# A table builder's back step cut in two inside an expert loop: four transposes move ahead of the second half of the token gathering

## Chip, cores and metric

The kernel runs on one core of a Trainium2 chip. The metric is device time in microseconds (us) of one execution; lower is better. Engines are named as in the profile: PE is TensorE's matmul, PEld its weight load, DVE is VectorE, ACT ScalarE, POOL GpSimd, SP SyncE, whose queue issues most of the transfers.

## The reference, cut to what matters

Two transformer blocks run one after the other on 512 tokens of width 1024. The first ends in a mixture of 32 experts, of which each token takes two; the second has an S5 layer (a state space model over 64 groups), whose tables follow from small parameters alone.

```python
y = (jax.nn.silu(xb @ w_gate[e]) * (xb @ w_up[e])) @ w_down[e]   # one expert; gate and up 1024x512, down 512x1024
...
b_bar = ((lam_bar - 1) / lam)[..., None] * lax.complex(b_re, b_im)   # S5, per group
a_pow = jnp.exp(lam_dt[None] * steps)
y = jnp.einsum('btgp,ghp->btgh', hs, c_mat).real
```

## The kernel before

**Expert stage.** `moe` walks through eight steps `st` of four experts, two pairs `pr` each, so 16 pairs; `eA` is the first expert of a pair and is 0 only for the first. For a pair PE makes the gate and up products `G` and `U` (L1032), turns the one-hot matrix (`pohT`, L1055), gathers tokens for the next step, turns the hidden values `hm` (`phT`, L1064, copied by ACT to `hT`, L1066), and makes the down products `Y` (L1081). The parts of the previous pair's result (`combine`, tile `pcmb`, L996 and L997) lie between the products. The first pair gathers nothing ahead, the second gathers four quarters, the pairs of the last step none, and each of the others two quarters: one before `phT` and one behind it. A quarter is 16 matmuls into one PSUM tile `pg` (L943, L944), which ACT moves out in two instructions to `xg` (L947). `pohT`, `pg` and `phT` take turns in a pool of two PSUM buffers.

**Weights.** SP issues them in the order of the program. A pair's ten tiles of 1 MB go through a ring of eight buffers (L129), and two more go to fixed places (`extra`, L970). A tile's transfer waits until the buffer's last reader on PE is done, and what is behind it on SP waits too: the last two `up` tiles of a pair wait for the `Y` before it.

**S5 tables.** The generator `s5_blocks` builds them in 16 half-blocks, in the shadow of the experts. Each half-block has three steps that end in a `yield`: loads by POOL (`Bd`, `cr`, `dd`, L1592 to L1597); maps (two small transposes `pcd`, and DVE's products `pb` and `m3`, which the profile names `m`); and the back step. The back step turns `pb` in four transposes into the PSUM tile `pm2` (L1628, `pm` in the profile), which ACT copies to `me` (L1629); then eight small products `pkt` (L1635) and one with the diagonal `dd` (L1637) go into a second tile, ACT copies that to `kt` (L1639), and POOL stores `me`, `m3` and `kt` (L1640 to L1642). `pm2` and `pkt` are taken from the same pool `psz` of one PSUM buffer, so the first `pkt` product waits for the copy of `pm2`.

**What sets the order.** In the expert stage PE's order is that of the program text: `pin` ties each matmul to the one before. On the other engines a scheduler orders by a simulation of its own and may take an instruction ahead of the text, as it does with DVE's product on `dd` (L1632). `pre` calls `next(self.blocks)` four times, so that half-block 0 is done and the loads of half-block 1 are out. The first pair then takes one step (maps of 1). Each pair after it takes two steps between the second quarter and `Y` (back, and the loads of the next half-block) and one behind `Y` (maps).

Of the kernel before, what the change touches and what calls it, by code (L numbers as in the profile page):

```python
# [71 lines left out]
def bcast_rows(ap, n):  # L72

    return bass.AP(tensor=ap.tensor, offset=ap.offset, ap=[[0, n]] + [list(x) for x in ap.ap])
# [24 lines left out]
class Build:  # L99
# [304 lines left out]
    def pre(self):  # L404
# [135 lines left out]
        for _ in self.side:  # L540
            pass
        self.ada_ctx.close()
        for _ in range(4):
            next(self.blocks)
        late = self.B((128, 4, D), name="late")
        g1 = late[:, 0]
# [402 lines left out]
    def moe(self):  # L949
# [29 lines left out]
        with ExitStack() as cx:  # L979
# [33 lines left out]
            for st in range(8):  # L1013
# [4 lines left out]
                for pr in range(2):  # L1018
                    eA = e0 + 2 * pr
# [39 lines left out]
                    half = len(quarters) // 2  # L1059
                    for q in quarters[:half]:  # L1060
                        self.gather(*q)
                    pt = self.psum(name="phT")
                    for k in range(4):
                        pin(nc.tensor.transpose(pt[:, k * 128:(k + 1) * 128], hm[:, k], self.ident))  # L1064
# [514 lines left out]
    def s5_blocks(self, sp, Pw, Qw, phc, cf):  # L1579
        nc, a = self.nc, self.a  # L1580
        tt, ts, stt = nc.vector.tensor_tensor, nc.vector.tensor_scalar, nc.vector.scalar_tensor_tensor
        flat = lambda ap: ap.rearrange("p a b c -> p (a b c)")
        PBT = lambda n: sp.tile([128, 4, 9, 16], F32, tag="s_pb", name=n, bufs=2)
        for hb in range(16):
            b, i = divmod(hb, 2)
            gs = slice(32 * i + 4 * b, 32 * i + 4 * b + 4)
            cols = lambda o: slice(o + i * 512, o + i * 512 + 512)

            Bd = sp.tile([128, 2, 4, 16], F32, tag="s_Bd", name="Bd", bufs=2)
            for j, nm in enumerate(("s5_b_re_2", "s5_b_im_2")):  # L1590
                for d in range(2):
                    nc.gpsimd.dma_start(Bd[64 * d:64 * d + 64, j], a[nm][0, gs].rearrange("g p h -> p g h"))  # L1592
            cr = sp.tile([64, 2, 64], F32, tag="s_cr", name="cr", bufs=2)
            for j, nm in enumerate(("s5_c_re_2", "s5_c_im_2")):
                nc.gpsimd.dma_start(cr[:, j], a[nm][0, gs].rearrange("g h p -> (g h) p"))
            dd = sp.tile([16, 4, 16], F32, tag="s_dd", name="dd", bufs=2)
            nc.gpsimd.dma_start(dd.rearrange("p g h -> p (g h)"), bcast_rows(a["s5_d_2"][0][gs.start * 16:gs.stop * 16], 16))  # L1597
            yield
            Cd = sp.tile([128, 2, 4, 16], F32, tag="s_Cd", name="Cd")
            pt = self.psum_z((64, 2, 64), name="pcd")  # L1600
            for j in range(2):
                self.pin(nc.tensor.transpose(pt[:, j], cr[:, j], self.ident[0:64, 0:64]))
            for d in range(2):
                nc.scalar.activation(Cd[64 * d:64 * d + 64].rearrange("p j g h -> p j (g h)"), pt, AF.Copy)

            Bb = sp.tile([128, 2, 4, 16], F32, tag="s_Bb", name="Bb")
            tmp = sp.tile([128, 4, 9, 16], F32, tag="s_tmp", name="tmpm")
            bt = flat(tmp)[:, 0:128].rearrange("p (j g h) -> p j g h", j=2, g=4)
            br, bi = [cf[:, j, None, gs, None].to_broadcast([128, 2, 4, 16]) for j in range(2)]
            tt(bt, Bd, bi, op=MUL)  # L1610
            tt(Bb, Bd, br, op=MUL)
            tt(Bb[:, 0], Bb[:, 0], bt[:, 1], op=SUB)
            tt(Bb[:, 1], Bb[:, 1], bt[:, 0], op=ADD)
            pb, m3 = PBT("pb"), PBT("m3")
            pbv = flat(pb)[:, 0:512].rearrange("p (g m h) -> p g m h", g=4, h=16)
            for dst, W, src, n in ((pbv, Pw, Bb, 8), (m3, Qw, Cd, 9)):
                w = [W[j][:, gs, :, None].to_broadcast([128, 4, n, 16]) for j in range(2)]
                x = [src[:, j, :, None, :].to_broadcast([128, 4, n, 16]) for j in range(2)]
                tm = tmp[:, :, 0:n]
                tt(dst, w[0], x[0], op=MUL)  # L1620
                tt(tm, w[1], x[1], op=MUL)
                tt(dst, dst, tm, op=SUB)
            yield

            me = sp.tile([128, 4, 128], F32, tag="s_me", name="me")
            pt = self.psum_z((128, 4, 128), name="pm2")
            for g in range(4):
                self.pin(nc.tensor.transpose(pt[:, g], pbv[:, g].rearrange("p m h -> p (m h)"), self.ident))  # L1628
            nc.scalar.activation(me, pt, AF.Copy)  # L1629

            kt = sp.tile([128, 4, 9, 16], F32, tag="s_tmp", name="kt")[0:16, :, 0:8]
            tt(dd, dd, self.ident[0:16, None, 0:16].to_broadcast([16, 4, 16]), op=MUL)  # L1632
            pk = self.psum_z((16, 4, 8, 16), name="pkt")
            for g in range(4):
                self.pin(nc.tensor.matmul(pk[:, g], pbv[:, g, 0, :], m3[:, g, 0:8, :], start=(g == 0), stop=False,  # L1635
                                          skip_group_check=True))
            self.pin(nc.tensor.matmul(pk[:, :, 0, :], self.ident[0:16, 0:16], dd, start=False, stop=True,  # L1637
                                      skip_group_check=True))
            nc.scalar.activation(kt, pk, AF.Copy)  # L1639
            nc.gpsimd.dma_start(self.s5d[b][0][:, cols(0)], me.rearrange("p g q -> p (g q)"))  # L1640
            nc.gpsimd.dma_start(self.s5d[b][1][:, cols(0)].rearrange("p (g m h) -> p g m h", g=4, h=16), m3[:, :, 1:9, :])
            nc.gpsimd.dma_start(self.s5k[b][4 * i:4 * i + 4, :, 7:15, :].rearrange("g h q o -> h g (q o)"),  # L1642
                                kt.rearrange("p g m o -> p g (m o)"))
            yield
# [498 lines left out]
```

## Time and profile before

| | |
|---|---|
| median of 3 runs | 2385.94 us (2385.44 to 2390.33) |
| profiled execution, its own time | 2385.08 us |
| its span, first to last instruction | 2383.3 us |
| PE busy | 2222.9 us, 93% of the span |
| DVE, ACT, POOL busy | 1363.7, 819.1, 237.1 us |
| mean granted clock of TensorE | 0.972 |
| experts in the trace, first `G` to last `Y` product | 432 to 979 us |

The span is 1.8 us shorter than the execution's time. In the rows below the first column of a timeline is the start in us from the span's start and the second the time from the start of the first to the end of the last of the merged instructions. What stands in brackets is how long the engine was idle ahead of them, and what ended that.

### The profile page before, as it was taken

The numbers are of one execution on the slowest core, as the hardware profiler recorded it, in microseconds if no ns is written. First come the engines' busy times: TensorE is split into PE (matmuls) and PEld (weight loads), VectorE is DVE, ScalarE is ACT, GpSimd is POOL, SyncE is SP. The second block draws the span as 40 slices with busy tenths as digits, with TensorE's granted clock in tenths as the row PEclk, the third lists the DMA queues.
The fourth block names the chain that finished last, engine by engine and source line by source line (L and its number), as shares of the span: only waits on it lengthen the run. The fifth ranks groups of instructions, "written<-read, shape, count | busy, mean of one in ns | idle before, by whom it ended". The sixth has DMA issues, their size and how long they took to land.

```text
span 2383.3 us, 32069 instructions
## 1 busy us (share of the span) xinstructions
PE 2222.9 (93%) x12448; PEld 1624.1 (68%) x12448; DVE 1363.7 (57%) x2585; ACT 819.1 (34%) x1321; POOL 237.1 (10%) x407
## 2 busy tenths in 40 slices
PE   7888997899999999898999999999999998999997
PEld 4665677454444444487697778897778777888887
DVE  4754565334433443648368874566786778544554
ACT  4222444121121121434243333346654434323332
POOL 0156000011111110100000000000121110000000
PEclk9889998899999999998999999999999999999998
DMA  8567225689999999756756763332333322233330
GB/s 290 161 199 236 72 72 208 235 339 386 374 380 389 369 376 397 260 159 195 239 163 208 242 208 98 97 110 76 103 115 89 107 80 89 73 95 97 97 98 36
DMA packets 254606, 454.02 MB, mean 191 GB/s; under 512 B 22596, under 2 KB 201556, under 8 KB 229876
## 3 DMA queue, kind: packets, MB, share of 16 engines
q1 hardware_dynamic: 245232, 435.25, 52.6%
q0 software_dynamic: 8464, 16.27, 2.1%
q8 instruction: 99, 1.62, 0.3%
q10 hardware_dynamic: 756, 0.43, 0.1%
q14 instruction: 55, 0.45, 0.1%
HBM read 436.15 MB, written 15.74 MB: 190 GB/s over the span
## 4 chain that ended last, share of the span: by engine, by line
PE 64%; DVE 7%; ACT 4%; DMA 3%; issue 2%; POOL 0%; SPq 0%; DVEq 0%; ACTq 0%; POOLq 0%
PE pt L157 13%; PE pt L158 12%; PE pt L159 12%; PE U L1032 5%; PE Y L1081 5%; PE G L1032 4%; DMA adaw<-in_ada_w 3%; PE pcmb L996 2%; PE pg L943 2%; PE pg L944 1%; PE pcmb L997 1%; DVE adaacc L325 1%; ACT wh L141 1%; DVE wl L142 1%; DVE q L1376 1%
## 5 line engine op out<-in xcount | busy, mean ns | idle before, releaser
L142 DVE TENSOR_TENSOR wl<-w,wh 128x1024 fp32r<-128x1024 f32 (+2 forms) x239 | 287.7, 1209 | 219.6 <-ACT wh L141 215.3
L141 ACT ACTIVATE wh<-w 128x1024 fp32r<-128x1024 f32 (+1 forms) x241 | 248.8, 1040 | 456.2 <-PE pt L158 362.8
L157 PE MATMUL pt<-hh,wh 128*128 128x512 f32 (+2 forms) x976 | 363.8, 378 | 3.2 <-ACT hh L1302 3.0
L158 PE MATMUL pt<-hl,wh 128*128 128x512 f32 (+2 forms) x976 | 362.5, 374 | 0.0
L159 PE MATMUL pt<-hh,wl 128*128 128x512 f32 (+2 forms) x976 | 360.6, 372 | 0.1
L157 PE MATMUL pt<-ab,wh 128*128 128x512 f32 (+1 forms) x576 | 211.2, 372 | 6.1 <-ACT o L1430 2.9
L158 PE MATMUL pt<-ab,wh 128*128 128x512 f32 (+1 forms) x576 | 212.0, 369 | 1.1 <-DVE ab L1379 0.9
L159 PE MATMUL pt<-ab,wl 128*128 128x512 f32 (+1 forms) x576 | 211.4, 368 | 0.0
L157 PEld LDWEIGHTS pt<-hh,wh 128*128 128x128 f32 (+1 forms) x976 | 181.8, 188 | 41.0 <-ACT hh L1302 4.0
L158 PEld LDWEIGHTS pt<-hl,wh 128*128 128x128 f32 (+1 forms) x976 | 182.6, 188 | 34.2 <-issue 3.3
L159 PEld LDWEIGHTS pt<-hh,wl 128*128 128x128 f32 (+1 forms) x976 | 183.0, 188 | 33.4 <-issue 1.7
L1410 DVE SCALAR_TENSOR_TENSOR x<-pt,mod,x 128x512 f32<-128x512 f32 (+1 forms) x184 | 122.1, 678 | 108.0 <-PE pt L159 107.6
L157 PEld LDWEIGHTS pt<-ab,wh 128*128 128x128 f32 x576 | 108.7, 191 | 29.9 <-ACT ab L1378 9.7
L158 PEld LDWEIGHTS pt<-ab,wh 128*128 128x128 f32 x576 | 109.9, 191 | 20.7 <-DVE ab L1379 3.4
L159 PEld LDWEIGHTS pt<-ab,wl 128*128 128x128 f32 x576 | 109.8, 191 | 17.4
L1032 PE MATMUL G<-w,xg 128*64 128x512 f32 x512 | 116.9, 599 | 0.0
L1032 PE MATMUL U<-w,xg 128*64 128x512 f32 x512 | 116.7, 598 | 0.0
L999 DVE TENSOR_TENSOR x<-x,pcmb 128x512 f32<-128x512 f32 x128 | 83.2, 682 | 55.1 <-PE pcmb L997 54.4
L2013 POOL TENSOR_TENSOR ec<-ec,BC 128x384 f32<-128x384 f32 x32 | 39.6, 1252 | 695.1 <-DMA bcs<-csd 544.0
L1632 DVE TENSOR_TENSOR dd<-dd,cst 16x64 f32<-16x64 f32 x16 | 3.4, 212 | 169.1 <-DMA dd<-in_s_d 141.4
L943 PE MATMUL pg<-oh,h2h 128*128 128x256 f32 x256 | 66.8, 297 | 21.2 <-DVE oh L930 12.4
L1032 PEld LDWEIGHTS U<-w,xg 128*64 128x64 f32 x512 | 34.1, 136 | 66.9 <-issue 62.2
(581 smaller groups left out, 4214.6 us busy)
## 6 DMA issues: line engine op xcount, KB each, us to landing
w<-in_w_gate SPq DMA_DIRECT2D x64, 1024.0 KB
w<-in_mlp_w SPq DMA_DIRECT2D x128, 512.0 KB
w<-in_w_up SPq DMA_DIRECT2D x63, 1024.0 KB
extra<-in_w_down SPq DMA_DIRECT2D x32, 1024.0 KB
w<-in_w_down SPq DMA_DIRECT2D x31, 1024.0 KB
adaw<-in_ada_w SPq DMA_DIRECT2D x48, 512.0 KB
adaw<-in_ada_w SPq DMA_DIRECT2D x96, 256.0 KB
w<-in_m_w_in SPq DMA_DIRECT2D x40, 512.0 KB
```

Of the source, the lines that this page charges most:

```text
L141: nc.scalar.activation(h, w, AF.Copy)
L142: (eng or nc.vector).tensor_tensor(l, w, h.bitcast(F32), op=SUB)
L157: nc.tensor.matmul(out, ah, bh, start=start, stop=False, skip_group_check=True)
L158: nc.tensor.matmul(out, ah, bl, start=False, stop=False, skip_group_check=True)
L159: return nc.tensor.matmul(out, al, bh, start=False, stop=stop, skip_group_check=True)
L943: self.pin(nc.tensor.matmul(pt[:, i], self.h2h[:, t, ks], oh2d[:, t], start=(t == 0), stop=False))
L996: pin(nc.tensor.matmul(pt, ls, yh[:, hf], start=True, stop=False))
L999: nc.vector.tensor_tensor(xs, xs, pt, op=ADD)
L1032: pin(nc.tensor.matmul(pt[64 * i:64 * i + 64], xg[:, kh * 4 + k, so + 64 * i:so + 64 * i + 64], ws[i][:, k], start=(kh == 0 and k == 0), s ...
L1081: pin(nc.tensor.matmul(Y[hf][64 * i:64 * i + 64], hT[:, 2 * kh + k, 64 * i:64 * i + 64], ws[i][:, k, hf * 512:(hf + 1) * 512], start=(kh = ...
L1410: self.nc.vector.scalar_tensor_tensor(xs, src, gate, xs, op0=MUL, op1=ADD)
L2013: nc.gpsimd.tensor_tensor(ec, ec, BC[:, 1, 128:512], op=MUL)
```

## The change

The back step gets a `yield` behind the copy of `pm2`, so that a half-block has four steps, and `pre` takes five in place of four, which leaves its work as it was. In each pair but the first, one step is now taken ahead of `phT`: the four transposes `pm2` and the copy to `me` stand between the first and the second half of the pair's gathering (where nothing is gathered, between `pohT` and `phT`). The products `pkt`, the copy to `kt`, the three stores and the next loads stay between the second quarter and `Y`.

```diff
@@ pre
-        for _ in range(4):
+        for _ in range(5):
             next(self.blocks)
@@ moe
                     for q in quarters[:half]:
                         self.gather(*q)
+                    if eA:
+                        next(self.blocks, None)
                     pt = self.psum(name="phT")
@@ s5_blocks
                 self.pin(nc.tensor.transpose(pt[:, g], pbv[:, g].rearrange("p m h -> p (m h)"), self.ident))
             nc.scalar.activation(me, pt, AF.Copy)
+            yield
 
             kt = sp.tile([128, 4, 9, 16], F32, tag="s_tmp", name="kt")[0:16, :, 0:8]
```

## Rows read from the trace of the kernel before

**Rows 1.** The profile's page: the chain that ended last, by engine
```profile
PE 64%; DVE 7%; ACT 4%; DMA 3%; issue 2%; POOL 0%; SPq 0%; DVEq 0%; ACTq 0%; POOLq 0%
```
**Rows 2.** Waits of PE, 440 to 1000 us: total us, times, longest
```profile
PE pkt L1635 <- ACT me L1629: 16.6, 15, 1.2
PE pg L943 <- ACT xg L947: 8.8, 13, 0.7
```
**Rows 3.** Timeline of PE, one pair; the last row is the next pair's
```profile
661.93 0.39 PE L943 MATMUL pg<-oh,h2h 128*128 128x256 f32 x1 [0.67 <-ACT xg L947]
...
663.83 0.28 PE L944 MATMUL pg<-oh,h2l 128*128 128x256 f32 x1
663.95 0.60 PE L1628 MATMUL pm<-cst,pb 128*128 128x128 f32 x4
665.71 1.05 PE L1635 MATMUL pkt<-m,pb 128*16 128x128 f32 x8 [1.16 <-ACT me L1629]
...
700.65 1.05 PE L1635 MATMUL pkt<-m,pb 128*16 128x128 f32 x8 [1.16 <-ACT me L1629]
```
**Rows 4.** Timeline of ACT, the same pair
```profile
660.86 1.02 ACT L947 ACTIVATE xg<-pg,ssp 128x256 f32<-128x256 f32 x2 [1.37 <-PE pg L944]
661.77 0.59 ACT L1066 ACTIVATE hT<-phT 128x512 f32<-128x512 f32 x1
664.15 1.02 ACT L947 ACTIVATE xg<-pg,ssp 128x256 f32<-128x256 f32 x2 [1.79 <-PE pg L944]
665.06 0.59 ACT L1629 ACTIVATE me<-pm 128x512 f32<-128x512 f32 x1
```
**Rows 5.** Timeline of the last pair, which gathers nothing
```profile
969.01 0.60 ACT L1058 ACTIVATE ohT<-pohT 128x512 fp32r<-128x512 f32 x1 [10.30 <-PE pohT L1055]
969.27 0.60 PE L1628 MATMUL pm<-cst,pb 128*128 128x128 f32 x4
969.50 0.59 ACT L1066 ACTIVATE hT<-phT 128x512 f32<-128x512 f32 x1
969.98 0.60 ACT L1629 ACTIVATE me<-pm 128x512 f32<-128x512 f32 x1
970.64 1.05 PE L1635 MATMUL pkt<-m,pb 128*16 128x128 f32 x8 [0.77 <-ACT me L1629]
...
975.31 3.60 PE L1081 MATMUL Y<-w,hT 128*64 128x512 f32 x16
```
**Rows 6.** Stretches: busy us of PE, PEld, DVE, ACT, POOL, then clock, DMA share, GB/s
```profile
658.60:693.50 34.90, 33.07 (x174) 15.94 (x173) 13.71 (x27) 6.49 (x13) 5.89 (x10) 1.00 0.97 378
672.00:673.00 1.00, 1.00 (x8) 0.33 (x6) 0.00 (x0) 0.00 (x0) 0.00 (x0) 1.00 1.02 418
673.00:674.00 1.00, 1.00 (x8) 0.19 (x4) 0.87 (x2) 0.03 (x1) 0.00 (x0) 1.00 0.42 172
674.00:675.00 1.00, 1.00 (x6) 0.40 (x8) 0.37 (x1) 0.60 (x1) 0.49 (x1) 1.00 0.20 49
969.00:970.00 1.00, 0.87 (x8) 0.63 (x6) 0.83 (x2) 0.99 (x3) 0.00 (x0) 1.00 0.38 152
```
**Rows 7.** Timeline of SP, the same pair as rows 3
```profile
657.36 17.45 SPq L129 DMA_DIRECT2D w<-in_w_up  x4
```
**Rows 8.** The chain, 640 to 720 us: PE's products of the next pair
```profile
677.80 0.43 PE pcmb L996
...
688.70 3.58 PE U L1032 x16
```
**Rows 9.** Timeline of POOL and DVE, the same pair
```profile
667.26 0.53 POOL L1597 DMA_DIRECT2D dd<-in_s_d  x1 [0.75 <-PE pkt L1637]
673.06 0.21 DVE L1632 TENSOR_TENSOR dd<-dd,cst 16x64 f32<-16x64 f32 x1 [13.32 <-DMA dd<-in_s_d]
673.20 0.73 DVE L1087 SCALAR_TENSOR_TENSOR y<-Y,wv,gt 128x512 f32<-128x512 f32 x1
...
676.68 0.69 DVE L1089 TENSOR_TENSOR yl<-y,yh 128x512 fp32r<-128x512 f32 x1 [0.70 <-ACT yh L1088]
```

## The prediction

> **What bounds the kernel now.** The page comes first: PE holds most of the chain that ended last and no other engine comes near it [rows 1]. What counts is therefore where PE stands still in the stage that the change touches, and so I read PE's waits from 440 to 1000 us next. Two of them matter: the first `pkt` product waits for ACT's copy to `me`, 15 times and 16.6 us in all, and the second quarter's first `pg` matmul waits for ACT's eviction of the first quarter, 13 times and 8.8 us [rows 2]. The reader is to see that these are both waits of PE for ACT, inside each pair, and that no weight transfer is in that list. Then come the timelines of one pair, which show the order behind the two waits [rows 3, 4]; one of the pairs that gather nothing [rows 5]; and the stretches, for how full the transfers are [rows 6]. The pairs follow each other very evenly: the same `pkt` product starts at 665.71 and at 700.65, a period of 34.94 us [rows 3]. The granted clock is 1.00 throughout [rows 6], so nothing here hangs on TensorE's clock.
>
> **The change, part by part.**
>
> *The fifth step in `pre`.* The text issues the same instructions in the same order as before; a `yield` emits none. Cost: nothing, with no cover needed.
>
> *The transposes, 13 pairs with gathering.* Before, PE stands still for 0.67 us between the end of `phT` and the second quarter's start at 661.93, since the first quarter's two evictions run from 660.86 to 661.88 [rows 3, 4]. The four transposes push `phT` back by at most the 0.60 us that they take from the first start to the last end, pipelined into what follows rather by less [rows 3], and that fits into 0.67. The second quarter waits for the evictions and not for PE, and these start when the first quarter ends, as before. So it still starts at 661.93, and the transposes are free. If that cover were gone they would cost up to 0.60 per pair, 8 us over 13.
>
> *What they leave behind.* The last `pg` matmul starts at 663.83, the transposes now there at 663.95 and the first `pkt` product at 665.71 [rows 3]. With `pm2` gone from here, and its copy done, the first product can take the place of the first transpose, at 663.95: 1.76 us earlier. That is the 0.60 of the transposes and the 1.16 of idle. If instead it had to wait until the modelled end of the last `pg` matmul (663.83 + 0.28 = 664.11), 1.60 would be left. I take 1.76, since the transposes that stand there now started at that spot with nothing in the way.
>
> *Is the copy done by then?* `pm2` would end some 0.6 us behind the first quarter, at 661.4. ACT is in the first quarter's evictions until 661.88, then copies `me` and `hT`, about 0.5 us apart as its rows start (969.50 and 969.98) [rows 4, 5]. Whichever goes first, both are done by 663.0, about 1 us ahead of the first `pkt` product and 2 us ahead of `Y`. What is queued behind `me` on ACT is `hT`, for which `Y` waits, and then the second quarter's evictions, which can't start before 664.15 anyway. Sum for these pairs: 13 x 1.76 = 22.9 us, with 13 x 1.60 = 20.8 as the lower bound.
>
> *The two pairs without gathering.* Here ACT sets the time: it copies `ohT`, `hT` and `me` one after the other, and `me` is last [rows 5]. With `pm2` ahead of `phT`, `me` takes the second place; it starts at 969.50 in place of 969.98, and `pkt` comes 0.48 us earlier. `hT` then ends at 970.6, while the products last until 971.3. The bounds are 0 (the order on ACT stays) and the whole wait of 0.77; I take 0.48 for each, 1.0 together.
>
> *Stores and loads.* The stores of `me`, `m3` and `kt` and the next loads stay in the second part. On POOL the store of `me` may go out some 3 us earlier than before; nobody waits for it in this stage. The load of `dd` waits for the `pkt` product that read the old one, and moves with it (a rival, below). POOL's queue has nothing else in these stretches.
>
> *Sum.* 22.9 + 1.0 = 23.9 us, from the profiled execution's own time: 2385.1 - 23.9 = 2361.2 us. That execution lies 0.9 us below the median, which is less than the runs differ among themselves. Behind the stage the chain goes on from the last pair's result, and I assume that it moves forward whole.
>
> *The weights, which now have less time.* Per period the transfers move 378 GB/s x 34.9 us = 13.2 MB. They run at 418 GB/s up to 673 and pause between 673 and 675, for 0.58 + 0.80 = 1.4 us [rows 6], because SP's last two `up` tiles wait for `Y` [rows 7]. So the transfers need about 33.5 us per period, and the new period of PE is 34.94 - 1.76 = 33.18 us. They would fall back by 0.3 us a pair, 4 us over 12 pairs. The tightest tile of a period is the second `up` half: SP is through with it at 674.81 [rows 7], 2.1 MB at 418 GB/s are 5 us, so it lands near 681, and it is wanted at 688.70 [rows 8]: 8 us to spare. At the end the weights' stream stops near 969.4 [rows 6], and the second half of the last `Y` wants its tiles at 975.31 [rows 5]: 6 us to spare, which is 2 us after a loss of 4. So I put no cost on it, but it is the closest call in this forecast. The DMA: Bandwidth & Descriptors page of the Trainium skill (Where 436 GB/s comes from) speaks against the change: it says that for loads from HBM the HBM's share of a core, about 358 GB/s, is the limit. By that, 13.2 MB are an estimated 36.9 us a pair, the weights would bound the stage already, and nothing would be gained. The trace disagrees: it has 378 GB/s over a whole period, and 418 within it.
>
> **The rivals.**
>
> *The weights become the bound (11 in 100).* For it: a share of 0.97, and a busy share is a rough measure of what is left. Against it: the spare time above. If the need were 34.4 us a period, 12 pairs would lose 14.6 us against PE, of which 8 are covered; 6.6 come back as waits on `U`: 2368 us. If no tile had any time to spare, the period would be 33.5 to 33.9, 1.4 to 1.0 us below that of before, and 13 pairs would bring 18.7 to 13.5 us: 2366 to 2372 us.
>
> *The weights are the bound already (1 in 100).* If each period waited for transfers, a shorter PE would only wait longer: 2385 us. The list of PE's waits has none for a tile of weights [rows 2], and the 8 us to spare stand against it.
>
> *The copy comes no earlier (5 in 100).* If the scheduler's order puts `me` behind the second quarter's evictions on ACT, it starts at 665.06 as before, and `pkt` at 665.71: the change would not do what it says, 2385 us within some 2 us. Against it: these evictions can't be ready until 2.5 us after the transposes are done, in a simulation too.
>
> *A late `dd` holds DVE (3 in 100, slower).* DVE's product on `dd` stands ahead of `y` in its queue and waits for a load that POOL issues behind `pkt`, at 667.26; it runs at 673.06 and `y` follows at once [rows 9]. If the scheduler gave that load a later place on POOL, or a fuller set of transfers made it slower, `y`, `yh`, `yl` and then `combine` would be late. The last `yl` ends at 677.37 and the combine parts begin at 677.80 [rows 8, 9], the ones that need it about 0.4 us later. So about 0.9 us are spare. Below that it costs nothing; to undo the gain, `dd` has to land 1.76 + 0.9 = 2.7 us later in each pair, and at 3.2 us it is slower: 15 x 0.5 = 8 us, 2393 us. For it: the wait is in every period. Against it: load and `Y` both start from the end of `pkt`, so their distance does not change. The same page of the Trainium skill (Issuing engines are not separate DMA queues) says that transfers of all issuing engines interleave on the same 16 DMA engines; so a small load can be slowed by the weights beside it. The row does not contradict that: 5.8 us passed from the issue to DVE's start.
>
> *A changed order elsewhere (5 in 100).* The scheduler's simulation shifts with the edit, and what follows the stage may be ordered otherwise on DVE, ACT or SP; some us either way, 2357 to 2375 us.
>
> **How the numbers follow.** The forecast as worked out has 75 in 100, with a range of its own from 2359 to 2365: at the lower end the 0.77 of the two last pairs whole and a run as low as the lowest shown, at the upper the lower bounds, 20.8 + 0 = 20.8, and a little for the spread. The range for 8 in 10 reaches into the case of the weights and some way into the last one: 2357 to 2369. About 0.2%, 5 us, is what a measurement of this kernel can tell from no change. The forecast (75), the weights that become the bound (11) and most of the changed order (4) are faster by more than that: 90. The weights that are it already, the copy that comes no earlier and the rest of the changed order are within it: 7. The late `dd`: 3.
>
> **What the profile after would show.** PE's wait of `pkt` for `me` is gone from the list, or down to some 0.3 us in the last two pairs. The wait of `pg` for `xg` stays, below 0.3 us long in place of 0.67. The same product's starts lie 33.2 us apart. ACT's `me` stands between the first quarter's evictions and `hT`. The transfers' pause of 1.4 us is gone or nearly so, with a mean near 397 GB/s. The forecast is wrong if a wait of `U`, `G` or `Y` for a weight transfer appears, if `me` starts behind 664, or if the last `combine` moves by less than the sum.

## The result, and the profile after

The changed kernel takes 2359.56 us (median of 4 runs, 2356.73 to 2363.59), the kernel before 2385.69 us beside it (4 runs, 2380.71 to 2390.33). The ratio is 0.9886, with an interval from 0.986 to 0.9911: 26.1 us, or 1.1%, faster. The forecast was 2361.2 us, the range 2357 to 2369. Three repeats (below) put the gain between 24.0 and 25.1 us. The profiled execution took 2362.38 us (span 2360.6 us, mean granted clock 0.971), 22.7 us less than that of before.

The program adds two lines at L1062 and one behind L1629, so `phT` is now L1066, `hT` L1068, `Y` L1083, `y` L1089, `pm` L1630, `me` L1631 and `pkt` L1638. PE and ACT have the same instructions as before but for the place of `pm2` and of `me`; the order of the other engines is unchanged.

First the chain that ended last, by engine, then the waits of PE from 430 to 1000 us (total us, times, longest), to be held against [rows 1, 2]:

```profile
PE 66%; DVE 7%; DMA 4%; ACT 3%; issue 2%; POOL 0%; SPq 0%; DVEq 0%; ACTq 0%; POOLq 0%
```

```profile
PE pg L943 <- ACT xg L947: 3.1, 13, 0.2
...
PE pkt L1638 <- ACT me L1631: 0.6, 2, 0.3
```

The wait of `pkt` for the copy went from 16.6 us to 0.6 us, and only the two pairs without gathering still have it. The wait of `pg` for the evictions went from 8.8 us to 3.1 us, since four transposes now stand inside it. No wait for a weight tile is in the list. The timeline of PE in one pair, with the next pair's `pkt` as its last row, against [rows 3]:

```profile
648.66 0.60 PE L1630 MATMUL pm<-cst,pb 128*128 128x128 f32 x4
649.10 0.60 PE L1066 MATMUL phT<-cst,hm 128*128 128x128 f32 x4
649.93 0.39 PE L943 MATMUL pg<-oh,h2h 128*128 128x256 f32 x1 [0.24 <-ACT xg L947]
650.16 0.28 PE L944 MATMUL pg<-oh,h2l 128*128 128x256 f32 x1
...
651.83 0.28 PE L944 MATMUL pg<-oh,h2l 128*128 128x256 f32 x1
652.03 1.05 PE L1638 MATMUL pkt<-m,pb 128*16 128x128 f32 x8
...
685.29 1.05 PE L1638 MATMUL pkt<-m,pb 128*16 128x128 f32 x8
```

The transposes push `phT` back by 0.44 us (648.66 to 649.10), and the wait in front of the second quarter is shorter by 0.43 us (0.67 to 0.24): they cost nothing. `pkt` follows the last `pg` matmul with no wait. Its starts lie 33.26 us apart, against 34.94 us. ACT in the same stretch, against [rows 4]:

```profile
648.86 1.02 ACT L947 ACTIVATE xg<-pg,ssp 128x256 f32<-128x256 f32 x2 [1.37 <-PE pg L944]
649.78 0.59 ACT L1631 ACTIVATE me<-pm 128x512 f32<-128x512 f32 x1
650.25 0.61 ACT L1068 ACTIVATE hT<-phT 128x512 f32<-128x512 f32 x1
```

The copy takes the place ahead of `hT` and is done at 650.37, 1.7 us before `pkt`. The last pair, against [rows 5]:

```profile
942.73 0.59 ACT L1631 ACTIVATE me<-pm 128x512 f32<-128x512 f32 x1
943.20 0.60 ACT L1068 ACTIVATE hT<-phT 128x512 f32<-128x512 f32 x1
943.37 1.05 PE L1638 MATMUL pkt<-m,pb 128*16 128x128 f32 x8 [0.28 <-ACT me L1631]
```

Here the wait is 0.28 us in place of 0.77. Last the stretches, against [rows 6] (busy us of PE, PEld, DVE, ACT, POOL, then granted clock, DMA share, GB/s): a whole period, and the two microseconds around the end of `Y`, where before the transfers paused.

```profile
652.30:685.56 33.26, 33.02 (x175) 16.00 (x173) 14.89 (x27) 6.50 (x14) 5.92 (x10) 1.00 1.01 400
659.00:660.00 1.00, 1.00 (x8) 0.14 (x2) 0.68 (x2) 0.28 (x1) 0.00 (x0) 1.00 1.03 426
660.00:661.00 1.00, 1.00 (x8) 0.39 (x8) 0.62 (x2) 0.35 (x1) 0.17 (x1) 1.00 0.98 410
```

The pause is gone and the mean rate has gone from 378 to 400 GB/s.

### The profile page after: what moved, and what is told of

It reads as the page before. It is cut to its first block, busy times and chain, and to the rows that moved or that the text cites. A ratio compares the mean times of both kernels' runs of the same rounds, so it can differ in the third digit from the quotient of the medians.

```text
span 2360.6 us, 32085 instructions
## 1 busy us (share of the span) xinstructions
PE 2227.2 (94%) x12448; PEld 1627.2 (69%) x12448; DVE 1361.9 (58%) x2585; ACT 819.6 (35%) x1321; POOL 239.4 (10%) x407
## 4 chain that ended last, share of the span: by engine, by line
PE 66%; DVE 7%; DMA 4%; ACT 3%; issue 2%; POOL 0%; SPq 0%; DVEq 0%; ACTq 0%; POOLq 0%
PE pt L157 13%; PE pt L158 12%; PE pt L159 12%; PE G L1032 5%; PE U L1032 5%; PE Y L1083 5%; DMA adaw<-in_ada_w 3%; PE pcmb L996 2%; PE pg L943 2%; PE pg L944 1%; PE pcmb L997 1%; DVE adaacc L325 1%; DVE wl L142 1%; ACT wh L141 1%; DVE q L1378 1%
```

## Experiments

Below, "stage" is the time from the first `pohT` transposes to the first `xp` transposes behind the experts: 535.95 us before, 513.12 us after. "Period" is the distance of two `pohT` starts, over the twelve in the middle of the stage; that of two `pkt` starts is the same there.

**Repeats of the changed kernel.** Each was timed beside the kernel before, on the same chip.

> The changed kernel once more, as the yardstick for the runs beside it. Both theories: 24 to 28 us below the kernel before (the expert stage alone was 23.6 us shorter in the two profiles), the first pkt products 33.26 us apart in the pairs that gather.

> The changed kernel as the yardstick of this group: 24 to 28 us below the kernel before.

> The changed kernel as the yardstick of this group: 24 to 28 us below the kernel before; from the first pohT to the first transposes behind the experts 513 to 514 us, as in its three profiles so far.

Measured: 2365.84 us against 2389.89 (0.9898, interval 0.9881 to 0.9914), 2363.70 against 2388.78 (0.989, 0.9864 to 0.9916) and 2365.03 against 2388.99 (0.9905, 0.9889 to 0.9921). The periods of the profiled executions are 33.26 to 33.27 us and the stages 513.1, 514.0 and 513.3 us, while their totals run from 2360.5 to 2372.1 us: nearly all of what differs between runs lies outside this stage.

**The transposes a step earlier**, ahead of the first quarter, where no wait stands that could hide them:

```
+                    if eA:
+                        next(self.blocks, None)
                     pt = self.psum(name="pohT")
...
-                    if eA:
-                        next(self.blocks, None)
                     pt = self.psum(name="phT")
```

> The four transposes pm2 go ahead of the whole gathering (before pohT) in place of its middle. Theory (the middle is worth it because the transposes lie there under the second quarter's wait for the eviction of the first): they cost their 0.44 us again in 13 pairs, the wait of pg for xg is back at 0.67 us, the period is 33.70 us, and the time is 5 to 6 us above the changed kernel, some 20 us below the one before. Rival 1 (all of the gain is the copy that is done in time, wherever the transposes stand): same as the changed kernel. Rival 2 (the weights set the period of 33.26 us by now): same too, with 0.44 us of waits less elsewhere.

Measured: 2372.48 us, ratio 0.9932 (0.9919 to 0.9946), 6.6 us above the changed kernel beside it. The period is 33.70 us, the stage 518.2 us, and PE's wait of `pg` for `xg` is back at 8.8 us in 13 times. So 0.44 us of the gain in each pair is the place of the transposes; a stage bound by weights would not have cared.

**A buffer of its own, order as before.** The kernel before, with `pkt` in another PSUM buffer than `pm2`, so that it need not wait for the copy:

```
-            pk = self.psum_z((16, 4, 8, 16), name="pkt")
+            pk = (self.psum if hb else self.psum_z)((16, 4, 8, 16), name="pkt")
```

> The kernel before, with the products pkt in the pool of two PSUM buffers in place of the one buffer that pm2 uses, from half-block 1 on. Theory (the wait of pkt for me is only that of the shared buffer): the 16.6 us of that wait go, nothing else does; the period is 33.78 us, pg still waits 0.67 us for xg, and the time is 16 to 17 us below the kernel before. Rival (the products would have to wait there for something else as well, the diagonal or a buffer): under 10 us below, with a new releaser in the list of PE's waits.

Measured: 2390.48 us, ratio 1.0006 (0.9995 to 1.0018). The expectation failed: the wait for the copy is gone, and nothing was gained. The periods are uneven, 34.65 to 36.27 us with a mean of 35.18, and PE has new waits, here from 430 to 1000 us (0.8 and 0.7 us of these two lines stand in the kernel before as well):

```profile
PE pcmb L996 <- ACT yh L1088: 4.4, 6, 0.8
PE pcmb L997 <- DVE yl L1089: 3.8, 16, 0.4
```

The combine parts wait for the result of `Y`, which comes late. Rows of PE, POOL and DVE from the timeline of one pair in the same kernel show why:

```profile
661.62 1.05 PE L1635 MATMUL pkt<-m,pb 128*16 128x128 f32 x8
663.79 0.53 POOL L1642 DMA_DIRECT2D s5k<-kt  x1
664.35 0.52 POOL L1597 DMA_DIRECT2D dd<-in_s_d  x1
669.83 0.30 PE L1602 MATMUL pcd<-cst,cr 64*64 64x64 f32 x2
670.66 0.21 DVE L1632 TENSOR_TENSOR dd<-dd,cst 16x64 f32<-16x64 f32 x1 [13.78 <-DMA dd<-in_s_d]
670.80 0.73 DVE L1087 SCALAR_TENSOR_TENSOR y<-Y,wv,gt 128x512 f32<-128x512 f32 x1
```

POOL issues the load of `dd` behind the store of `kt` now, 1.7 us behind the end of the eight `pkt` products in place of 0.5 [rows 3, 9], and 6.3 us pass from there to DVE's product in place of 5.8. DVE's product on `dd` waits for it and runs 0.83 us behind `pcd`, which marks the end of `Y`; `y`, next in DVE's queue, waits behind it. This is the prediction's rival of the late `dd`, in another kernel.

**The same, with the product on `dd` out of the way**: DVE does it at the end of the maps step, behind `y`:

```
-            yield
+            yield tt(dd, dd, self.ident[0:16, None, 0:16].to_broadcast([16, 4, 16]), op=MUL) if hb > 2 else None
...
-            tt(dd, dd, self.ident[0:16, None, 0:16].to_broadcast([16, 4, 16]), op=MUL)
-            pk = self.psum_z((16, 4, 8, 16), name="pkt")
+            if hb < 3: tt(dd, dd, self.ident[0:16, None, 0:16].to_broadcast([16, 4, 16]), op=MUL)
+            pk = (self.psum if hb else self.psum_z)((16, 4, 8, 16), name="pkt")
```

> The kernel before with the products pkt in a buffer of their own, as in the run own_buffer, and DVE's product on dd moved from the back step into the maps step, which stands behind yl, from half-block 3 on. Theory (in own_buffer the wait for the copy was gone but the later load of dd held DVE ahead of y, and the combine parts waited): period 33.70 us, no wait of pcmb for yh or yl inside the stage, 16 to 17 us below the kernel before. Rival (what came back in own_buffer has another cause, such as the kt copy or the buffer): within 5 us of the kernel before, periods uneven between 34.6 and 36.3 us.

Measured: 2371.59 us, ratio 0.9922 (0.9906 to 0.9939), so 17.2 us faster than before. Each of the twelve periods is 33.70 us, and the new waits of `pcmb` are gone. Its timeline has the load at the same late place, but `y` no longer behind the product:

```profile
662.99 0.52 POOL L1597 DMA_DIRECT2D dd<-in_s_d  x1
666.87 0.75 DVE L1087 SCALAR_TENSOR_TENSOR y<-Y,wv,gt 128x512 f32<-128x512 f32 x1 [11.35 <-PE Y L1081]
671.38 0.20 DVE L1623 TENSOR_TENSOR dd<-dd,cst 16x64 f32<-16x64 f32 x1
```

The late `dd` on DVE's queue, and nothing else, had taken the gain away. Matmul by matmul, three pairs of the run before this one are 0.99, 2.37 and 2.57 us longer than the same pairs here, and all of it lies at the combine parts. The list of waits shows less than that, since it counts idle time from the modelled ends of pipelined matmuls only. 33.70 us is also the period of the transposes a step earlier: both kernels drop the wait for the copy and leave the 0.67 us of the second quarter's wait unused.

**A shorter eviction.** The changed kernel, with the second eviction of each first-half tile on DVE, to shorten the 0.24 us that is left of the wait:

```
-                        self.gather(*q)
+                        self.gather(*q, dve=(1,))
...
+                nc.vector.tensor_scalar(xg[:, k], pt[:, i], self.sc2[:, k:k + 1], self.sh2[:, k:k + 1], op0=MUL, op1=ADD) if i in dve else ...
```

> The changed kernel, with the second of the two evictions of each gathering tile in the first half done by DVE in place of ACT, so that the two run side by side. Theory (what is left of the wait of pg for xg is 13 times 0.24 us of ACT's second eviction): that wait goes, the period is 33.02 us, 3 us below the changed kernel. Rival (the weights, which fill the transfers wholly in the changed kernel, set 33.2 us a pair): no change that can be measured, and waits of PE for a weight tile towards the end of the stage.

Measured: 2366.72 us, ratio 0.9893 (0.9875 to 0.9912), which can't be told from the changed kernel beside it. The expectation failed: the period is 33.39 us, 0.13 worse, and the wait in front of the second quarter is 0.36 us in place of 0.24. The two evictions did not overlap:

```profile
652.96 0.56 ACT L947 ACTIVATE xg<-pg,ssp 128x256 f32<-128x256 f32 x1 [1.37 <-PE pg L944]
653.56 0.55 DVE L947 TENSOR_SCALAR xg<-pg,ssp 128x256 f32<-128x256 f32 x1 [1.72 <-ACT xg L947]
654.16 0.39 PE L943 MATMUL pg<-oh,h2h 128*128 128x256 f32 x1 [0.36 <-DVE xg L947]
```

DVE's starts 0.04 us after ACT's has ended. The two read one PSUM tile and write one buffer; which of the two made DVE wait was not tried. About the weights this run says nothing.

**The two parts exchanged.** The changed kernel, with `pkt` and its copy between the quarters and `pm2` behind the second, from half-block 1 on:

```
+            def turn():
+                me = ...; pt = self.psum_z((128, 4, 128), name="pm2")
+                (the four transposes, the copy to me)
+                return me
+            if hb == 0: me = turn(); yield
...
             nc.scalar.activation(kt, pk, AF.Copy)
+            if hb: yield; me = turn()
```

> The changed kernel with the two parts of the back step exchanged from half-block 1 on: the products pkt (1.25 us on PE) and the copy to kt between the two halves of the gathering, the transposes pm2 and the copy to me behind the second. Theory (only cover counts: 1.25 us and phT are more than the 1.1 us that the evictions take, and nothing on PE waits for the copy to me): the 0.24 us of pg's wait go in 13 pairs too, the period is 33.02 us, 3 us below the changed kernel. Rival (the weights, whose transfers fill the period wholly now, set 33.2 us): no change that can be measured, with waits of U or G for a weight tile.

> The kernel of the run swap once more, with five rounds beside the changed kernel. Theory (the 0.35 us a pair that its profile showed reach the end): 3 to 6 us below the changed kernel, and 508 us from the first pohT to the first transposes behind the experts. Rival (given back behind the stage): the stage is shorter by that and the time is the same or above.

Measured: 2362.55 us (0.989, 0.9871 to 0.9909) and 2358.54 us (0.9874, 0.9854 to 0.9894), 1.2 and 6.5 us below the changed kernel beside it. Its median is the lowest of the full kernels in both groups, but its interval overlaps that of the changed kernel in both, so the totals alone do not show that it is faster. The stage does: 507.9 and 510.3 us against 514.0 and 513.3 beside it, with a period of 32.91 us in both profiles. (The first pair, which stands ahead of the twelve periods, took 1.7 us longer in the second profile, and so it did in that of the changed kernel in the first group; in both, 3.4 us of it ran at a granted clock of 0.50.) One pair, PE and then the stretch of one period:

```profile
652.87 1.05 PE L1638 MATMUL pkt<-m,pb 128*16 128x128 f32 x8
...
654.05 0.66 PE L1066 MATMUL phT<-cst,hm 128*128 128x128 f32 x4
654.47 0.37 PE L943 MATMUL pg<-oh,h2h 128*128 128x256 f32 x1
...
685.77 1.05 PE L1638 MATMUL pkt<-m,pb 128*16 128x128 f32 x8
```

```profile
653.40:686.30 32.90, 32.90 (x174) 15.94 (x173) 14.97 (x27) 6.59 (x14) 5.90 (x10) 1.00 1.02 404
```

The products are long enough to fill the wait for the evictions, and PE does not stand still at all in this pair. The period fell by 0.35 us where 0.24 was expected. Here the second quarter starts 0.42 us behind the first transpose of `phT` (654.05, 654.47), and in the changed kernel 0.83 us behind it (649.10, 649.93). So the wait cost 0.41 us there. The profile's 0.24 counts from the modelled end of the transposes, with which the next matmul overlaps when it need not wait. Some 0.06 us is lost again where other instructions now follow each other.

**Less work for PE**, to find the weights' own limit: the changed kernel without the low-half matmuls of the gathering, so the low part of the gathered tokens is left out.

```
-                    self.pin(nc.tensor.matmul(pt[:, i], self.h2h[:, t, ks], oh2d[:, t], start=(t == 0), stop=False))
-                    self.pin(nc.tensor.matmul(pt[:, i], self.h2l[:, t, ks], oh2d[:, t], start=False, stop=(t == 3)))
+                    self.pin(nc.tensor.matmul(pt[:, i], self.h2h[:, t, ks], oh2d[:, t], start=(t == 0), stop=(t == 3)))
```

> The changed kernel without the second product of the gathering (the low halves h2l, L944), which leaves out that part of the tokens; nothing is changed in the weights. 16 matmuls less per pair, 1.9 us of PE. Theory (the transfers need some 33.2 us a pair and the tiles had 8 us to spare): the period is 31.3 us at first and returns to about 33.2 once the spare time is used up, with waits of PE for weight tiles; 10 to 18 us below the changed kernel. Rival (the transfers could go faster, their full share is only queued packets): 31.3 us to the end, some 30 us below the changed kernel, no such waits.

Measured: 2347.77 us, ratio 0.9826 (0.9807 to 0.9844). That is 15.9 us below the changed kernel beside it, inside the 10 to 18 expected. The periods are uneven, 31.37 to 34.09 us with a mean of 32.35. Waits of PE and of its weight load in the stage (`U` is L1031 here), and one stretch:

```profile
PEld U L1031 <- DMA w<-in_w_up: 9.2, 10, 1.8
...
PE U L1031 <- DMA w<-in_w_up: 1.5, 3, 0.9
```

```profile
773.00:805.00 32.00, 31.67 (x153) 14.52 (x151) 15.03 (x27) 5.63 (x12) 5.91 (x10) 1.00 1.02 405
```

Now `U` waits for its weights: the transfers are the bound, at about 32.4 us a period on average. The theory was right in kind, but its limit of 33.2 us was too high.

**The transposes behind `phT`**, in the changed kernel:

```
-                    if eA:
-                        next(self.blocks, None)
                     pt = self.psum(name="phT")
...
+                    if eA:
+                        next(self.blocks, None)
                     hT = mp.tile([128, 4, 128], F32, tag="sg", name="hT", bufs=1)
```

> The changed kernel with the transposes pm2 behind phT in place of ahead of it, still in front of the second quarter. Theory (only what lies under the wait of pg for xg counts, not the order there): the period of the gathering pairs is 33.26 us as in the changed kernel, and in the two pairs without gathering pkt waits 0.7 to 0.8 us for me again, as in the kernel before. Rival (the place ahead of phT matters, since ACT now copies hT before me and Y or pkt come later): a longer period, by up to the 0.6 us of one copy.

Measured: 2366.95 us in its one run, a period of 33.26 us, and for the two last pairs a wait of `pkt` for `me` of 1.5 us in two times (0.8 the longest) in place of 0.6. In the gathering pairs the order of the two groups of transposes is nothing; in the last two it is about the 0.48 us each that the prediction named.

## Why the prediction was right

**The free transposes: right.** The row of the wait (0.24 us) shows it, and the run with the transposes a step earlier shows the other side: without the cover they cost 0.44 us a pair; the bound of 0.60 took them as not pipelined.

**The copy in time: right**, in the order `xg`, `me`, `hT`, as worked out.

**1.76 us a pair: the right mechanism, a term a little too large.** The rows give 34.94 - 33.26 = 1.68 us. The first product starts 0.20 us behind the last `pg` matmul; I let it start 0.12 us behind, as the transposes did. Over 13 pairs that is 21.8 us in place of 22.9. The two last pairs gave 0.47 and 0.51 us, with 0.48 forecast. The 1.68 us is 0.44 for the transposes, which the run with the transposes a step earlier lacks, and 1.24 for the wait, which the run with `dd` out of the way gained alone (34.94 - 33.70).

**A term that the sum lacked.** From the first `pohT` to the last `pkt` the profiles give 519.88 - 496.24 = 23.6 us, and 21.8 + 1.0 is only 22.8. The other 0.9 us comes from two pairs of before that were not like the others, with periods of 35.39 and 35.37 us. In both, `dd` came late. The first of them, in the trace of before:

```profile
737.13 0.53 POOL L1597 DMA_DIRECT2D dd<-in_s_d  x1 [0.75 <-PE pkt L1637]
743.78 0.30 PE L1602 MATMUL pcd<-cst,cr 64*64 64x64 f32 x2
744.07 0.21 DVE L1632 TENSOR_TENSOR dd<-dd,cst 16x64 f32<-16x64 f32 x1 [14.46 <-PE pcd L1602]
```

Load to product took 6.9 us here, not 5.8 [rows 9], and the product ran behind the end of `Y`. The row names `pcd`, whose signal came last, but in the trace the load landed at 743.98, the usual 0.1 us ahead of the product: the last of its 16 signals came 1.2 us behind the fifteenth. Nearly all of the 0.45 us that each of the two lost stands at the combine parts, as with the buffer of its own. The prediction called the periods very even, and so counted no gain there; after, all twelve are 33.26 us. Why the load was slow in those two pairs is open. That the sum of 23.9 us came so near to 23.6 is luck in part: 1.1 us too much in one term and 0.9 us left out nearly cancel.

**The weights cost nothing: right, but their need was too high.** The prediction took 33.5 us a period from 34.9 less the 1.4 us pause, although its own 13.2 MB at the 418 GB/s of rows 6 are only 31.6 us. The changed kernel's period is below that, and PE never waits for weights. Exchanged parts run at 32.91 us with 404 GB/s and no wait for weights in the twelve periods (one of 0.2 us ahead of them); with less work on PE the limit shows, at about 32.4 us, between the two figures. 13.2 MB at the 405 GB/s seen there are 32.6 us. So the expected loss of 0.3 us a pair was none. The rule of the Trainium skill that stood against the change (DMA: Bandwidth & Descriptors, Where 436 GB/s comes from) does not hold for this kernel, which runs on one core: 400 GB/s over a whole period, above its 358.

**The late `dd`: did not happen, and is a real price.** After, the load goes out 0.3 us behind the last product of the second tile, as before, and DVE's product stands ahead of the end of `Y` (`pcd`, 660.24):

```profile
653.59 0.53 POOL L1599 DMA_DIRECT2D dd<-in_s_d  x1 [2.36 <-PE pkt L1640]
658.81 0.21 DVE L1635 TENSOR_TENSOR dd<-dd,cst 16x64 f32<-16x64 f32 x1 [11.06 <-DMA dd<-in_s_d]
```

The buffer of its own, in which the load did take a later place, lost 35.18 - 33.70 = 1.5 us a pair by it.

**The rest of the total.** In the two profiles the first `pohT` starts at 450.8 us before and at 447.1 us after, though the instructions up to there are the same; the stage gives 22.8 us; and 3.7 us are lost again behind it. The granted clock differs the same way: 0.913 before and 0.920 after ahead of the stage, 0.981 and 0.977 behind it. Ahead of the stage, and just behind the last pair, the stretches of before and then of after are:

```profile
100.00:200.00 100.00, 87.41 (x624) 62.64 (x624) 54.10 (x196) 26.28 (x45) 48.00 (x119) 0.88 0.62 199
983.00:988.00 5.00, 4.52 (x22) 2.91 (x23) 4.31 (x9) 2.90 (x5) 0.00 (x0) 1.00 0.77 199
```

```profile
100.00:200.00 100.00, 89.32 (x659) 63.19 (x659) 57.54 (x208) 29.58 (x53) 51.13 (x121) 0.93 0.68 213
956.00:961.00 5.00, 5.00 (x17) 2.94 (x18) 3.68 (x6) 2.23 (x5) 0.00 (x0) 0.66 0.70 175
```

From 100 to 200 us the granted clock was 0.93 after and 0.88 before. In the combine parts behind the last pair it was 0.66 after, 3.4 us of it at the lower level of 1.2 GHz, and 1.00 before, which is where the stage's 23.6 us became 22.8. The run with the buffer of its own, which gained nothing, has 3.4 us at that level there too, so it does not come with the gain alone. Counted from the first `pohT`, the last combine parts thus move by 22.8 us, less than the sum of 23.9, which the prediction named as a sign of being wrong: 0.3 us of that is the sum's error and 0.8 the clock here. The four groups' medians differ by 24 to 26 us, 1 to 3 more than the stage. The stage's figure lies inside the interval of each (0.9881 to 0.9914, that of the first repeat, is 20.6 to 28.4 us). The mean granted clocks of the groups' executions, 0.971 after and 0.971 to 0.972 before, do not explain it, so where it comes from is open; that the forecast lay within 2 us of a median is partly luck.

## What to carry to other kernels

Where two steps share one PSUM buffer and the copy between them stalls TensorE, put independent work between them, and best put the first step inside a wait that stands there anyway: that alone made 33.26 us of 33.70. Before taking a wait away, look which loads it releases on another queue and what stands in order behind their consumer; a product on DVE's queue that waited for a small late load ate 1.5 us a pair. For the reserve of a stream of weights do not go by the share of time that it is busy. The bytes over the highest rate in sight gave 31.6 us here, the period less the pause 33.5, and the limit that was measured, 32.4, lies between them.

## What the hardware showed beyond that

The transfers' busy share was a poor measure of what was left: at 0.97 (378 GB/s) the rate could still rise by 7%, at 1.01 (400) and 1.02 (404) by about 1% or less, to the 405 GB/s at which PE waited. A wait of TensorE behind four transposes cost 0.41 us where the profile's idle time says 0.24, because idle time counts from the modelled end of pipelined work. Four transposes pushed the next instruction of PE back by 0.42 to 0.53 us, not by the 0.60 to 0.66 from their first start to their last end. Evictions of two parts of one PSUM tile by ACT and DVE into one buffer ran one behind the other (0.04 us between them), where side by side was expected.
